# Gate-up groups of a feed-forward layer: the upper right product last, the next group's first split behind the result additions

## The chip, the cores and the metric

The kernel runs on one core of a Trainium2 chip. The metric is the device time of one execution in microseconds (us); lower is better. The core's engines work side by side, each through its own queue in order: TensorE (PE; its weight loads are shown as PEld), VectorE (DVE), ScalarE (ACT), GpSimd (POOL) and SyncE (SP). They wait for one another by semaphores. Matrix products are accumulated in PSUM, eight banks of 128 x 512 numbers; VectorE and ScalarE read and write these banks too. Operands lie in SBUF, and transfers from HBM are issued by SP and POOL.

## The reference

One layer of an encoder on x of 256 x 2048, all in float32:

```
x = x + 0.5 * post1(SwiGLU_1(pre1(x)))      # feed-forward, inner width 5632
h = pre_m(x);  p = h @ W_in                  # one projection
x = x + post_m(concat(HGRN2(p), attention(p)) @ W_out)
x = x + 0.5 * post2(SwiGLU_2(pre2(x)))      # feed-forward again

def swiglu(x, w_gate_up, w_down):
    gate, up = jnp.split(x @ w_gate_up, 2, axis=-1)
    return (jax.nn.silu(gate) * up) @ w_down
```

The change lies in `x @ w_gate_up`, a product of 256 x 2048 by 2048 x 11264, which is there twice, once for each feed-forward layer. With the gate and up halves read side by side, it is worked on in groups of columns.

## The kernel before, in words

**Numbers in two parts.** TensorE takes float32 operands in a rounded form. So each weight is split: ScalarE casts it to a rounded part h (L176), and VectorE subtracts this from the weight and leaves a rest l (L177). A product is then three matmuls, h by the large part of x, l by the large part, h by the small part (`three`, L441). A split of half a loaded weight tile is one cast and one subtraction of 128 x 1024. The h and l tiles come from pools of five buffers each, so a cast waits until TensorE is done with an older tile.

**Groups.** A group of `Gated` is 512 columns of gate and the same 512 of up, for all 256 rows and all 2048 inner places. There are NG = 11 groups to a layer, 0 to 10. Inside a group the inner places come in eight pairs u = 0 to 7 (two blocks of 128 each). A group has four results in four PSUM banks: c[m][n], where m is the upper or lower 128 rows and n is gate (left) or up (right).

**Plain pairs and seven-product pairs.** A plain pair needs eight block products, so 24 matmuls. Some pairs (`MIXED_IN`: u = 2, 4, 5, 6; in group 1 only 2 and 4) are worked on with seven block products instead of eight, by a scheme of sums and differences like Strassen's (`products`, L485). That is 21 matmuls, and they use sums of weight blocks (VectorE, L915 and L916, and an accumulating transfer that POOL issues in `prepare`, L901) and sums of x blocks (xs). Three of the seven products go straight into the result banks c[0][0], c[0][1] and c[1][0]; four go into four more banks: p1, p5 (tag pa), p6 and p7 (tag pb). All pairs of a group add into the same banks. The seven, in the order of the code, are: p1; c[0][0]; c[0][1], the upper right one; p5; p7; p6; c[1][0], the lower left one. The first needs its own split (prepared much earlier), the second and third need the split called `lower`, the fourth and fifth `upper`, the last two `last`.

**The boundary.** At the end of a group the four p banks have to be added into the four results. This is `boundary(g)` (L1101), for groups 1 to 9 of each layer, 18 times in the kernel. By then the last seven-product pair (u = 6) is queued on TensorE, and pair 7, a plain one, is still to do. Its products are queued bank by bank (`bank`, L1108): the six matmuls of a bank stand behind the addition into this bank. In order: ScalarE copies p1 (L1112); VectorE adds it to c[0][0] (L1113); L1116 and L1117 form sums with p6 and p7; L1118 adds to c[1][0]; L1121 and L1122 form a difference with p5 and add to c[0][1]; L1124 and L1125 do the same for c[1][1]. TensorE works the banks in the order c[0][0], c[1][0], c[0][1], c[1][1], and then begins pair 0 of the next group.

Between L1113 and L1116 the first half of the next group's pair 0 is split (`ahead = gated.splits(g + 1, 0)`, `next(ahead)`); the second half is split at the end, behind L1125.

**After it.** ScalarE computes silu of the gate results (L1039) and VectorE the product with the up results (L1044), spread over the next group's first pairs. In some groups (2 to 5 of each layer) finished tiles of this are stored to HBM (`put_away`), since they don't all fit; the stores stand in SP's queue among the loads.

**What sets the order.** All of this stands under a manual schedule: the order of the Python calls is the order of the queues. A weight tile's buffer is loaded again (`load_next`) when its last split is done; for pair 0 that is behind the second half.

In the text, the boundaries are numbered 0 to 17 in order of time: 0 to 8 in the first layer, 9 to 17 in the second.

Of the kernel before, what the change touches and what calls it, by code (L numbers as in the profile page):

```python
# [24 lines left out]
KT = D // P  # L25
# [12 lines left out]
def hymba_layer_kernel(  # L38
# [41 lines left out]
    def pa():  # L80
        return psum.tile([P, 512], F32, tag="pa", name=nm("pa"))

    def pb():
        return psum.tile([P, 512], F32, tag="pb", name=nm("pb"))
# [130 lines left out]
    last = {}  # L215
# [20 lines left out]
    def take(*a):  # L236
        take_hi(*a)
        take_lo(*a)
# [59 lines left out]
    def proj_T_pieces(w, c0, xt, slot, khs=(0, 1), parts=None):  # L298

        for i, kh in enumerate(khs):  # L300
# [26 lines left out]
            for n, (products, at) in enumerate(steps):  # L327
                products(*at)
                if n % 4 == 3:
                    yield  # L330
# [71 lines left out]
    class Blocks:  # L402
# [4 lines left out]
        ahead = None  # L407
# [74 lines left out]
            last = split_half(raw, 1)  # L482
            self.products(u, first, lower, upper, last)

        def products(self, u, first, lower, upper, last):  # L485

            if not self.p:
                self.p = [pa(), pa(), pb(), pb()]
            a, w = self.tiles[u], self.left_sums(u)

            def lhs(k, m):
                return [a[:, k, i, m * P : (m + 1) * P] for i in range(2)]

            def summed(j):
                return [w[:, j, i, :] for i in range(2)]

            def rhs(two, n):
                return [x[:, n * 512 : (n + 1) * 512] for x in two]

            for at, left, right in (  # L500
                (("p", 0), lhs(0, 0), first),
                (("c", 0, 0), lhs(1, 0), rhs(lower, 0)),
                (("c", 0, 1), summed(S4), rhs(lower, 1)),
                (("p", 1), summed(S1), rhs(upper, 0)),
                (("p", 3), summed(S3), rhs(upper, 1)),
                (("p", 2), summed(S2), rhs(last, 1)),
                (("c", 1, 0), lhs(1, 1), rhs(last, 0)),
            ):
                self.three(at, *left, *right)

        def fold(self):
# [78 lines left out]
    class Pairs(Blocks):  # L590
# [93 lines left out]
        def finish(self, mul, post, new_x=None, gain=None, lead=None):  # L684
# [45 lines left out]
            if gain is None:  # L730
# [8 lines left out]
                with tc.manual_schedule(engines=ordered):  # L739
                    products(0, 0, every)  # L740
                    squares(0, 0)
                    gains(0, 0)
                    products(0, 1, every)
                    squares(0, 1)
                    gains(0, 1)
                    products(1, 0, every)
                    squares(1, 0)
                    for q in range(4):
                        update(0, q)
                    in_place(0)  # L750
                    products(1, 1, every)
                    squares(1, 1)
                    in_place(1)
                    for q in range(4):
                        store(0, q)
                    update_aside(1, 0)
                    for q in (1, 2, 3):
                        update(1, q)
                        store(1, q)
                    store(1, 0)  # L760
# [82 lines left out]
    NG = DFF // 512  # L843
# [11 lines left out]
    class Gated(Blocks):  # L855
# [73 lines left out]
        def take(self, g, u):  # L929

            got = self.split_of.pop((g, u))
            del self.raws[g, u]
            first = self.firsts.pop((g, u), None)
            if first:
                self.products(u, first, *got)
                return ()
            hs, ls = zip(*got)
            return [
                (lambda k=k, m=m, n=n: self.plain(u, hs, ls, m, n, k))
                for k in range(2)  # L940
                for m in range(2)
                for n in range(2)
            ]
# [27 lines left out]
    def ffn(gated, w_dn, post_gain, again, gain=None, lead=None, aside=None):  # L971

        with ExitStack() as st:
# [9 lines left out]
            def room_for(tag):  # L983
                return work.tile([P, 512], F32, tag=tag, name=nm(tag))
# [97 lines left out]
            def some(steps, n):  # L1082
                for _ in range(n):
                    next(steps)

            pre_stats()
            last = KT // 2 - 1
# [13 lines left out]
            def boundary(g):  # L1101

                a, b = room_for("z"), room_for("s")
                c, (p1, p5, p6, p7) = gated.c, gated.p
                add = nc.vector.tensor_tensor
                rest_of = gated.take(g, last)

                def bank(m, n):  # L1108
                    for k in range(2):
                        rest_of[4 * k + 2 * m + n]()  # L1110

                nc.scalar.copy(a, p1)  # L1112
                add(c[0][0], c[0][0], a, ALU.add)  # L1113
                ahead = gated.splits(g + 1, 0)
                next(ahead)
                add(b, p6, a, ALU.add)  # L1116
                add(a, p7, b, ALU.add)  # L1117
                add(c[1][0], c[1][0], a, ALU.add)  # L1118
                bank(0, 0)
                bank(1, 0)  # L1120
                add(b, p5, b, ALU.subtract)  # L1121
                add(c[0][1], c[0][1], b, ALU.add)  # L1122
                bank(0, 1)
                add(b, p5, a, ALU.subtract)  # L1124
                add(c[1][1], c[1][1], b, ALU.add)  # L1125
                bank(1, 1)
                next(ahead)

            def first_pairs(g, waiting):

# [36 lines left out]
            with tc.manual_schedule():  # L1167
                gated.prepare(1, MIXED_IN[0])
                some(gated.splits(1, 0), 2)
                for g in range(1, NG):  # L1170
                    first_pairs(g, waiting)
                    for u in range(2, last - 1):
                        pair_ahead(g, u)
                    if g < NG - 1:
                        ahead = gated.splits(g, last)
                        some(ahead, 2)
                        gated.prepare(g + 1, MIXED_IN[0])
                        for one in gated.take(g, last - 1):
                            one()
                        boundary(g)  # L1180
                        waiting = units(gated.c, rest)
                        some(waiting, 2)
# [47 lines left out]
    def two_banks():  # L1230
        return [[pa(), pa()], [pb(), pb()]]

    gated = Gated(w_ffn1_gate_up[0], two_banks())
    xt = new_xt()
    gated.see(xt)
    with tc.manual_schedule():
# [5 lines left out]
        def taken(m, q, js=range(4)):  # L1242
            take(m, q, gain1, xt, banks[m, q], js)
# [3 lines left out]
        first = gated.source(0)  # L1247
# [120 lines left out]
    with ExitStack() as s2:  # L1368
# [227 lines left out]
        def gates(half):  # L1596

            sl = [pa(), pa()]
            for _ in proj_N_pieces(w_in, 4096 + half * 512, 512, xt, sl):
                side_step()  # L1600
            g = mid.tile([P, 2, 512], F32, tag="g", name=nm("g"))
            for m in range(2):
                by = rs2[:, m : m + 1]
                nc.scalar.activation(g[:, m, :], sl[m], AF.Sigmoid, scale=by)
                nc.vector.scalar_tensor_tensor(g[:, m, :], sl[m], by, g[:, m, :], ALU.mult, ALU.mult)
            return g
# [129 lines left out]
        for hp in range(4):  # L1736
            zf = headpair(2048 + hp * 256, "zf")
            if hp == 1:
                g = gates(0)
# [18 lines left out]
        g = gates(1)  # L1758
# [13 lines left out]
        gated = Gated(w_ffn2_gate_up[0], two_banks())  # L1772
# [80 lines left out]
```

## Time and profile before

| | |
|---|---|
| median of 3 runs | 1850.8 us (1848.57 to 1854.73) |
| the profiled execution | 1851.23 us; its span, first to last instruction, 1849.5 us |
| TensorE busy | 1816.7 us, 98% of the span |
| VectorE busy | 1628.2 us, 88% |
| ScalarE busy | 1127.2 us, 61% |
| moved by DMA | 422.42 MB, 228 GB/s on average |
| granted TensorE clock | 0.999 of full speed |

The gate-up groups with boundaries last from about 60 to 480 us in the first layer and from about 1185 to 1605 us in the second. How to read the rows: a group such as "DVE L177 TENSOR_TENSOR l<-raw,h" names the engine, the line, the operation, and what is written from what. In an answer in order of time, each row begins with its start and its length in us; xN means so many instructions like it, and square brackets give the idle time of this engine ahead of it and what ended it. In an answer on waits, the numbers are the sum, the count and the longest. A matmul's end is modelled, 0.39 us behind its start, while the next one starts 0.227 us behind it; so starts are compared here. The idle time that the profile gives for TensorE counts from such modelled ends, and is shorter than the delay of the start.

### The profile page before, as it was taken

The page shows a single profiled execution, that of the slowest core. Times are in us where ns is not written, and L with a number is a line of the kernel's source. Part 1 is how long each engine was busy: PE and PEld are TensorE (multiplying, and loading weights), DVE is VectorE, ACT ScalarE, POOL GpSimd, SP SyncE. Part 2 cuts the span into 40 slices and gives each one's busy share as a digit, 9 for nine tenths or more (in the row PEclk, how much of TensorE's full clock was granted, in tenths as well). Part 3 has the DMA queues.
Part 4 walks back from the last instruction along what each step waited for, and adds up shares of the span by engine and source line. Part 5 has one row for each costly group of instructions (what it writes and reads, how often), then busy time and mean ns, then how long its engine had stood idle before and what let it go on. Part 6 is the DMA issues. An engine that isn't in the chain of part 4 may idle for free.

```text
span 1849.5 us, 23264 instructions
## 1 busy us (share of the span) xinstructions
PE 1816.7 (98%) x8438; PEld 1504.2 (81%) x8438; DVE 1628.2 (88%) x2071; ACT 1127.2 (61%) x1492; POOL 114.3 (6%) x115
## 2 busy tenths in 40 slices
PE   9999999999999999999999999999999999999998
PEld 7877878888887888888888888878888778888886
DVE  7999999998999999477687788899999999999897
ACT  7565556655665557477587556555666556666563
POOL 1011111111000000000000000011111111000000
PEclk9999999999999999999999999999999999999999
DMA  8789999888756566656554456789999888865565
GB/s 298 228 219 275 274 268 256 247 244 251 272 186 226 196 248 211 208 175 181 166 171 148 169 212 245 220 237 262 272 272 254 255 246 237 262 236 206 183 237 183
DMA packets 200020, 422.42 MB, mean 228 GB/s; under 512 B 10984, under 2 KB 45888, under 8 KB 199136
## 3 DMA queue, kind: packets, MB, share of 16 engines
q1 hardware_dynamic: 178880, 380.95, 59.9%
q0 software_dynamic: 21024, 39.99, 12.9%
q8 instruction: 66, 1.08, 0.2%
q14 instruction: 50, 0.41, 0.1%
HBM read 408.29 MB, written 12.60 MB: 228 GB/s over the span
## 4 chain that ended last, share of the span: by engine, by line
PE 70%; DVE 14%; DMA 8%; ACT 4%; issue 3%; SPq 1%; POOL 0%; DVEq 0%; ACTq 0%; POOLq 0%
PE pa L441 28%; PE pb L441 25%; DVE l L177 8%; DMA raw<-in_w_ffn_gate_up_dram 6%; PE pa L309 5%; PE pa L314 3%; ACT h L176 3%; PE pa L364 2%; PE pa L363 2%; PE pa L362 2%; DMA raw<-in_w_ffn_down_dram 2%; DVE pb L1118 1%; DVE z L1117 1%; DVE pa L1113 1%; DVE s L1116 1%
## 5 line engine op out<-in xcount | busy, mean ns | idle before, releaser
L176 ACT CAST h<-raw 128x1024 fp32r<-128x1024 f32 (+1 forms) x861 | 846.7, 1013 | 454.2 <-PE pb L441 113.2
L177 DVE TENSOR_TENSOR l<-raw,h 128x1024 fp32r<-128x1024 f32 (+1 forms) x861 | 985.0, 1170 | 136.8 <-ACT h L176 105.5
L441 PE MATMUL pa<-h,xt 128*128 128x512 f32 x1104 | 387.5, 392 | 0.2
L441 PE MATMUL pb<-h,xt 128*128 128x512 f32 x952 | 341.1, 393 | 17.5 <-DVE pb L1118 17.5
L441 PEld LDWEIGHTS pa<-h,xt 128*128 128x128 f32 x1104 | 207.4, 188 | 44.3 <-DVE xt L232 0.6
L441 PEld LDWEIGHTS pb<-h,xt 128*128 128x128 f32 x952 | 178.6, 188 | 64.4 <-DVE pb L1118 25.1
L441 PE MATMUL pa<-l,xt 128*128 128x512 f32 x552 | 215.7, 391 | 0.0
L441 PE MATMUL pb<-l,xt 128*128 128x512 f32 x476 | 185.5, 390 | 0.0
L441 PE MATMUL pb<-h,ht 128*128 128x512 f32 x464 | 163.5, 390 | 0.0
L441 PE MATMUL pa<-h,ht 128*128 128x512 f32 x464 | 162.7, 389 | 0.0
L901 POOL DMA_DIRECT2D raw<-in_w_ffn_gate_up_dram x76 | 92.0, 1211 | 758.1 <-DVE l L177 709.1
L309 PE MATMUL pa<-xt,h 128*128 128x512 f32 x512 | 124.4, 392 | 0.2 <-ACT h L176 0.2
L441 PEld LDWEIGHTS pa<-l,xt 128*128 128x128 f32 x552 | 103.9, 188 | 20.6 <-DVE l L177 0.7
L309 PEld LDWEIGHTS pa<-xt,h 128*128 128x128 f32 x512 | 93.8, 188 | 18.6 <-ACT h L176 0.6
L441 PE MATMUL pa<-h,xs 128*128 128x512 f32 x304 | 105.9, 389 | 0.0
L441 PE MATMUL pb<-h,xs 128*128 128x512 f32 x304 | 105.9, 389 | 0.0
L441 PEld LDWEIGHTS pb<-l,xt 128*128 128x128 f32 x476 | 89.4, 188 | 17.1
L441 PEld LDWEIGHTS pa<-h,ht 128*128 128x128 f32 x464 | 87.1, 188 | 18.2
L441 PEld LDWEIGHTS pb<-h,ht 128*128 128x128 f32 x464 | 87.1, 188 | 18.1
L441 PE MATMUL pb<-l,ht 128*128 128x512 f32 x232 | 90.3, 389 | 0.0
L441 PE MATMUL pa<-l,ht 128*128 128x512 f32 x232 | 90.3, 389 | 0.0
L314 PE MATMUL pa<-xt,l 128*128 128x256 f32 x512 | 69.1, 285 | 0.0
(289 smaller groups left out, 2517.6 us busy)
## 6 DMA issues: line engine op xcount, KB each, us to landing
raw<-in_w_ffn_gate_up_dram SPq DMA_DIRECT2D x350, 512.0 KB, 5.3
raw<-in_w_ffn_down_dram SPq DMA_DIRECT2D x88, 1024.0 KB, 5.2
raw<-in_w_mix_in_dram SPq DMA_DIRECT2D x52, 1024.0 KB, 5.0
raw<-in_w_ffn_gate_up_dram POOLq DMA_DIRECT2D x76, 512.0 KB, 8.3
raw<-in_w_mix_out_dram SPq DMA_DIRECT2D x16, 1024.0 KB, 5.0
away<-ht SPq DMA_DIRECT2D x16, 512.0 KB, 6.6
ht<-away SPq DMA_DIRECT2D x16, 512.0 KB, 7.4
pg<-in_post_norm_ffn_dram SPq DMA_DIRECT2D x4, 512.0 KB, 6.8
```

The costliest lines, as they stand in the source:

```text
L176: nc.scalar.copy(hi, src)
L177: nc.vector.tensor_tensor(lo, src, hi.bitcast(F32), ALU.subtract)
L309: nc.tensor.matmul(slot[f], weights(hs, kk, f), xcol(xt, k), start=(k == 0), stop=(k == KT - 1))
L314: nc.tensor.matmul(slot[f][:, 0:T], weights(ls, kk, f), xcol(xt, kh * 8 + kk, 0), start=False, stop=False,)
L362: nc.tensor.matmul(dst, xh, h[:, o : o + n], start=(k == 0), stop=False)
L363: nc.tensor.matmul(dst, xh, l[:, o : o + n], start=False, stop=False)
L364: nc.tensor.matmul(dst, xl, h[:, o : o + n], start=False, stop=(k == KT - 1))
L441: nc.tensor.matmul(self.bank(at), lhs, rhs, start=(n == 1), stop=n in (ends, self.of[at]), skip_group_check=n > ends,)
L901: nc.gpsimd.dma_start(raw[:, 0:1024].rearrange("p (k c) -> p k c", k=2), self.source(u, g)[:, :, 1], accum_op=ALU.add,)
L1113: add(c[0][0], c[0][0], a, ALU.add)
L1116: add(b, p6, a, ALU.add)
L1117: add(a, p7, b, ALU.add)
```

## The change

Two things change places, and no instruction is added or removed.

- In the last seven-product pair of a group (u = 6, in groups 2 to 9), the upper right product, which was third of the seven, comes last. The others keep their order: p1, c[0][0], p5, p7, p6, c[1][0], c[0][1].
- In `boundary`, the split of the next group's first half, which stood between L1113 and L1116, comes behind the last of the additions, directly ahead of the split of the second half.

```diff
-        def products(self, u, first, lower, upper, last):
+        def products(self, u, first, lower, upper, last, order=range(7)):
...
-            for at, left, right in (
+            seven = (
                 (("p", 0), lhs(0, 0), first),
                 (("c", 0, 0), lhs(1, 0), rhs(lower, 0)),
                 (("c", 0, 1), summed(S4), rhs(lower, 1)),
...
                 (("c", 1, 0), lhs(1, 1), rhs(last, 0)),
-            ):
+            )
+            for i in order:
+                at, left, right = seven[i]
                 self.three(at, *left, *right)
...
             if first:
-                self.products(u, first, *got)
+                before_fold = g < NG - 1 and u == KT // 2 - 2
+                self.products(u, first, *got, (0, 1, 3, 4, 5, 6, 2) if before_fold else range(7))
                 return ()
...
                 nc.scalar.copy(a, p1)
                 add(c[0][0], c[0][0], a, ALU.add)
-                ahead = gated.splits(g + 1, 0)
-                next(ahead)
                 add(b, p6, a, ALU.add)
...
                 add(c[1][1], c[1][1], b, ALU.add)
                 bank(1, 1)
-                next(ahead)
+                some(gated.splits(g + 1, 0), 2)
```

In the changed file the lines of `boundary` lie lower: L1112 to L1113 become L1115 to L1116, and L1116 to L1125 become L1117 to L1126.

## The prediction

> **What bounds the kernel now.** I read the page first (busy time, slices, chain), then who waits for line L1118, then one group boundary in order of time, then stretches of groups.
>
> ```profile
> PE 1816.7 (98%) x8438; PEld 1504.2 (81%) x8438; DVE 1628.2 (88%) x2071; ACT 1127.2 (61%) x1492; POOL 114.3 (6%) x115
> ...
> PE   9999999999999999999999999999999999999998
> ...
> DVE  7999999998999999477687788899999999999897
> ...
> PE 70%; DVE 14%; DMA 8%; ACT 4%; issue 3%; SPq 1%; POOL 0%; DVEq 0%; ACTq 0%; POOLq 0%
> ```
>
> TensorE is the bound at 98%, and 70% of the chain that ended last is its work; VectorE has 14%. In the first and the last third, which hold the gate-up groups of the two feed-forward layers, VectorE is at 9 tenths as well. One of its lines there makes TensorE wait:
>
> ```profile
> L1118 DVE TENSOR_TENSOR pb<-pb,z x18: 700/700/700, 96.9 to 1565.7; 128x512 f32<-128x512 f32 x18
> ...
>   PE pb L441: 17.5, 18
> ```
>
> Each of the 18 boundaries stops TensorE once, until the lower left result has its addition (L1118). One boundary (number 5 of 0 to 17; 0 to 8 lie in the first layer) in order of time:
>
> ```profile
> 306.39 0.39 PE L441 MATMUL pa<-h,xt 128*128 128x512 f32 x1
> ...
> 308.67 1.05 ACT L176 CAST h<-raw 128x1024 fp32r<-128x1024 f32 x1
> ...
> 309.49 0.69 DVE L1113 TENSOR_TENSOR pa<-pa,z 128x512 f32<-128x512 f32 x1
> ...
> 309.99 1.05 ACT L176 CAST h<-raw 128x1024 fp32r<-128x1024 f32 x1 [0.26 <-PE pb L441]
> ...
> 310.09 1.22 DVE L177 TENSOR_TENSOR l<-raw,h 128x1024 fp32r<-128x1024 f32 x1
> ...
> 310.24 0.39 PE L441 MATMUL pb<-h,xs 128*128 128x512 f32 x1
> ...
> 310.92 0.39 PE L441 MATMUL pb<-h,xt 128*128 128x512 f32 x1
> ...
> 311.15 0.39 PE L441 MATMUL pa<-h,xt 128*128 128x512 f32 x1
> ...
> 311.22 0.68 DVE L1116 TENSOR_TENSOR s<-pb,z 128x512 f32<-128x512 f32 x1
> ...
> 312.74 0.70 DVE L1118 TENSOR_TENSOR pb<-pb,z 128x512 f32<-128x512 f32 x1
> ...
> 313.49 0.50 PE L441 MATMUL pb<-h,xt 128*128 128x512 f32 x1 [0.82 <-DVE pb L1118]
> ...
> 314.06 0.70 DVE L1122 TENSOR_TENSOR pa<-pa,s 128x512 f32<-128x512 f32 x1
> ...
> 315.00 0.39 PE L441 MATMUL pa<-h,xt 128*128 128x512 f32 x1
> ...
> 315.52 0.70 DVE L1125 TENSOR_TENSOR pb<-pb,s 128x512 f32<-128x512 f32 x1
> ...
> 315.58 0.69 ACT L1039 ACTIVATE z<-pa,scales 128x512 f32<-128x512 f32 x1 [4.54 <-DVE s L1124]
> ...
> 316.13 1.21 DVE L177 TENSOR_TENSOR l<-raw,h 128x1024 fp32r<-128x1024 f32 x1
> ...
> 316.37 0.40 PE L441 MATMUL pb<-h,xt 128*128 128x512 f32 x1
> ...
> 317.26 0.74 DVE L1044 SCALAR_TENSOR_TENSOR z<-pa,scales,z 128x512 f32<-128x512 f32 x1
> ...
> 317.77 0.39 PE L441 MATMUL pa<-h,xt 128*128 128x512 f32 x1
> ```
>
> The pair's 21 matmuls issue from 306.39 to 311.15: 0.227 us each. A result bank then takes six, 1.36 us. The upper left bank starts at 311.15, so the lower left one could start at 312.51; it starts at 313.49, 0.98 us late. VectorE runs without a break from L1113 on, and the next group's first split (310.09) stands in it ahead of L1116. That split isn't needed before 317.77.
>
> **The change, part by part.** Nothing is added or removed; seven products and eight VectorE operations change places.
>
> The split behind the additions: L1113 to the split is 0.60 us from start to start, the split to L1116 1.13. Taking it out brings L1116, L1117, L1118, L1121, L1122, L1124 and L1125 forward by 1.13, if their operands are there. L1118 then ends at 313.44 - 1.13 = 312.31, ahead of TensorE's 312.51, so this wait goes. The next banks start every 1.36: 313.87, where L1122 has ended at 314.76 - 1.13 = 313.63, and 315.23, where L1125 has ended at 316.22 - 1.13 = 315.09. The new group starts at 316.59 instead of 317.77. TensorE's ceiling is 1.18 and VectorE's 1.13; I take 1.13, since margins of 0.14 to 0.24 less semaphore time leave nothing over.
>
> The row and the Trainium skill differ slightly on this price. Its page "VectorE: DVE Perf Modes", section "The DRAIN you can't avoid", says that the next VectorE operation starts only when the one before has emptied the pipe. By that the removed split is worth its whole 1.22, capped by 1.18, and the sum below would be some 0.5 us larger; the trace does not quite agree: L1116 starts at 311.22, before 310.09 + 1.22.
>
> The product order: the sixth product's last matmul (310.24, ends 310.63) comes 0.68 earlier, to 309.95, before L1116's new start 309.49 + 0.60 = 310.09. The seventh (310.92, ends 311.31) ends at 310.63, before L1118's new 311.61. Without this half of the change L1116 would wait from 310.09 to 310.63, so 0.5 of the 1.13 hangs on it where VectorE is on time. The upper right product, now last, ends at 311.31 and is wanted at 314.06 - 1.13. TensorE's time is the same in any order. This half applies from the second boundary of each layer on (16 of 18); at the two others the pair is plain and its products lie far back.
>
> What is moved past what: the casts of the first two splits (308.67, 309.99) take the room of earlier operands, and in the new order wait for the fourth and the sixth product, ending near 310.4 and 311.8. ScalarE idles 4.54 before 315.58, and the split that reads the first now starts near 315.0: nothing. The split must end before the group's second matmul, at 316.59 + 0.23; it ends near 316.2. The second split stays at 316.13, so the load that reuses that buffer (SP) is issued as before, and POOL's accumulating loads and all VectorE work from 317.26 on keep their times. What is late next is therefore VectorE, against a TensorE that is 1.13 further.
>
> Does each group keep it? That depends on what lies between two boundaries. Stretches from L1113 to L1113, of one, four and three groups (columns: stretch, length, busy time and count of PE, PEld, DVE, ACT, POOL, then clock, DMA share, GB/s):
>
> ```profile
> 93.60:136.60 43.00, 41.66 (x188) 34.10 (x187) 40.00 (x49) 25.80 (x31) 4.81 (x4) 1.00 0.85 228
> 136.60:309.50 172.90, 168.43 (x753) 137.68 (x753) 159.41 (x190) 102.92 (x121) 19.35 (x16) 1.00 0.93 268
> 309.50:438.10 128.60, 126.13 (x565) 103.32 (x565) 118.78 (x139) 77.53 (x90) 14.52 (x12) 1.00 0.88 245
> ```
>
> ScalarE's waits for loads in the second of them, and then in the third (sum, times, longest):
>
> ```profile
> ACT h L176 <- DMA raw<-in_w_ffn_gate_up_dram: 24.0, 12, 3.9
> ...
> ACT h L176 <- DMA raw<-in_w_ffn_gate_up_dram: 2.6, 3, 1.0
> ```
>
> And a group of the third in order of time:
>
> ```profile
> 331.78 1.05 ACT L176 CAST h<-raw 128x1024 fp32r<-128x1024 f32 x1 [0.99 <-PE pa L441]
> ...
> 332.87 1.22 DVE L177 TENSOR_TENSOR l<-raw,h 128x1024 fp32r<-128x1024 f32 x1 [0.82 <-ACT h L176]
> ...
> 343.11 2.59 DVE L177 TENSOR_TENSOR l<-raw,h 128x1024 fp32r<-128x1024 f32 x2 [0.81 <-ACT h L176]
> ```
>
> In the third stretch a group takes 42.87 us and VectorE works 39.6 of it. Its idle (0.82, 0.81) is behind casts which wait for TensorE to free their buffers (331.78): it follows TensorE. With 41.7 us a group VectorE still has 2.1 to spare, so these groups pass the lead on. So does the first stretch (40.0 of 43.0), the group after boundary 0, and its like after boundary 9.
>
> In the second stretch, where results are stored to HBM beside the loads, casts wait 24.0 us for weights. The chain there is load, cast, VectorE without a break, boundary, next load, and TensorE's earlier start doesn't shorten it. Each boundary takes 1.13 out again, but such a group first takes back the lead that TensorE had from the boundary before. It leaves only VectorE's idle that follows TensorE after the last wait for a load:
>
> ```profile
> 148.80 1.22 DVE L177 TENSOR_TENSOR l<-raw,h 128x1024 fp32r<-128x1024 f32 x1 [2.45 <-ACT h L176]
> ...
> 214.20 2.59 DVE L177 TENSOR_TENSOR l<-raw,h 128x1024 fp32r<-128x1024 f32 x2 [0.40 <-ACT h L176]
> ...
> 300.24 2.59 DVE L177 TENSOR_TENSOR l<-raw,h 128x1024 fp32r<-128x1024 f32 x2 [0.24 <-ACT h L176]
> ...
> 1295.45 2.59 DVE L177 TENSOR_TENSOR l<-raw,h 128x1024 fp32r<-128x1024 f32 x2 [0.23 <-ACT h L176]
> ...
> 1338.30 2.59 DVE L177 TENSOR_TENSOR l<-raw,h 128x1024 fp32r<-128x1024 f32 x2 [0.63 <-ACT h L176]
> ...
> 1381.19 2.58 DVE L177 TENSOR_TENSOR l<-raw,h 128x1024 fp32r<-128x1024 f32 x2 [0.57 <-ACT h L176]
> ```
>
> Of the eight such groups (after boundaries 1 to 4 and 10 to 13), five have 0.40, 0.24, 0.23, 0.63 and 0.57; the other three have none (148.80 is a load's). Sum 2.07. Bounds for the eight: 0, if the store and load traffic grows denser with shorter groups, and 8 x 1.13 = 9.0, if loads move forward with the work.
>
> The sum: boundaries 0 and 9 give 1.13 each; each group after them adds what it passes on. Full: 2 boundaries + 8 groups (after 0, 5, 6, 7 and after 9, 14, 15, 16) = 10 x 1.13 = 11.3; load-paced: 2.1. Together 13.4 us. The profiled execution took 1851.23 (span 1849.5), so 1837.8; the runs' median, 1850.8, is 0.4 lower: 1837.4.
>
> **The rivals.**
> *All boundaries keep theirs.* 18 x 1.13 = 20.3, 1830.5. For it: many loads are issued when VectorE frees a buffer, so a part could come earlier. Against it: the 24.0 us of waits for loads.
> *VectorE and the loads take back more.* VectorE's share would rise from 92% to 95% (39.6 of 41.7), with accumulating loads between. If the eight load-paced groups give nothing and the eight others half, 2 x 1.13 + 4.5 = 6.8: 1844.0. Against it: the idle of 0.82 and 0.81 behind TensorE.
> *No change.* Every group needs room freed by TensorE (331.78). If the boundary's wait only mirrors scarce room, an earlier start would be waited off at the next buffer, and 1850.8 stays. Against it: a split stands in front of L1118, without idle between. The Trainium skill, "Perfetto Trace Analysis", section "Optimization Strategy", says that the same gap repeating on the engine that should be saturated can mean too little room for the next tile; by that reading this rival holds, and the trace does not bear it out here, since the wait ends with an addition.
> *Slower.* The first split is now behind L1125, and TensorE needs it two matmuls into the group. If it ended 0.62 late, TensorE would wait there instead; every us more is paid up to 18 times. It loses 0.3% when the split ends 0.62 + 1.13 + 0.31 late, by a late cast or addition: 18 x 0.31 = 5.6, 1856.4. Against it: the cast is done 3 us before, and L1125's operands lie ready.
>
> **How the numbers follow.** Forecast 0.58, all kept 0.12, taken back 0.18, no change 0.06, slower 0.06. What this kernel's runs can tell from no change is about 0.3%, 5.6 us. Faster by more than that: 0.58 + 0.12 and nearly all of "taken back", 0.85. Within: 0.09; slower: 0.06. The range goes from all kept (1830.5, rounded down) to taken back with a microsecond for the spread of the runs (1845); its ends hold the bounds of the load-paced groups (11.3 and 20.3 us).
>
> **What would show it.** Right: L1119 (once L1118) makes TensorE wait near zero at boundaries 5 to 8 and 14 to 17, whose groups take 41.7 us; the four groups after boundary 1 keep about 43; casts there still wait some 24 us for loads. Wrong: waits of TensorE behind L177 or the group's first split; groups of 42.9 after boundary 5; or those four groups shorter by 4 us or more in all (then all is kept).

## The result, and the profile after

The changed kernel took 1835.8 us (median of 4 runs, 1835.46 to 1840.23), and the kernel before, on the same chip, 1852.8 (4 runs, 1848.57 to 1855.65): a ratio of 0.9916, 95% interval 0.9889 to 0.9942. A second comparison, beside the last of the experiments, gave 1838.6 (6 runs, 1835.99 to 1844.24) against 1851.1, a ratio of 0.9936 (0.9922 to 0.995). The profiled execution took 1835.46, with a span of 1833.7 where before's was 1849.5: 15.8 us less. It is the fastest of its runs, as the profiled one of the second comparison was; the ten runs together have a median of 1837.7, where 1837.4 was forecast.

The page of the changed kernel: busy time, the chain that ended last, and two groups of instructions (busy and mean ns, then the idle time ahead of them).

```profile
PE 1815.3 (99%) x8438; PEld 1503.5 (82%) x8438; DVE 1626.8 (89%) x2071; ACT 1125.7 (61%) x1492; POOL 114.4 (6%) x115
...
PE 72%; DVE 15%; DMA 6%; ACT 3%; issue 3%; SPq 0%; POOL 0%; DVEq 0%; ACTq 0%; POOLq 0%
...
L176 ACT CAST h<-raw 128x1024 fp32r<-128x1024 f32 (+1 forms) x861 | 843.9, 1013 | 472.2 <-DMA raw<-in_w_ffn_gate_up_dram 92.4
...
L441 PE MATMUL pb<-h,xt 128*128 128x512 f32 x952 | 340.9, 393 | 2.6 <-DVE pb L1119 2.4
```

The busy times are those of before to within 1.5 us. What has gone is TensorE's idle time ahead of the lower left bank: 17.5 us before, 2.4 now. The addition into that bank, L1119 now, made TensorE wait at seven boundaries instead of 18:

```profile
L1119 DVE TENSOR_TENSOR pb<-pb,z x18: 699/700/700, 95.6 to 1550.0; 128x512 f32<-128x512 f32 x18
...
  PE pb L441: 2.4, 7
```

Boundary 6 of the changed kernel in order of time, VectorE first and then TensorE's first matmul of each bank and of the new group:

```profile
346.65 0.69 DVE L1116 TENSOR_TENSOR pa<-pa,z 128x512 f32<-128x512 f32 x1
347.25 0.68 DVE L1117 TENSOR_TENSOR s<-pb,z 128x512 f32<-128x512 f32 x1
...
348.76 0.70 DVE L1119 TENSOR_TENSOR pb<-pb,z 128x512 f32<-128x512 f32 x1
...
351.62 0.70 DVE L1126 TENSOR_TENSOR pb<-pb,s 128x512 f32<-128x512 f32 x1
352.22 2.35 DVE L177 TENSOR_TENSOR l<-raw,h 128x1024 fp32r<-128x1024 f32 x2
```

```profile
348.31 0.39 PE L441 MATMUL pa<-h,xt 128*128 128x512 f32 x1
...
349.67 0.39 PE L441 MATMUL pb<-h,xt 128*128 128x512 f32 x1
...
351.04 0.39 PE L441 MATMUL pa<-h,xt 128*128 128x512 f32 x1
...
352.43 0.43 PE L441 MATMUL pb<-h,xt 128*128 128x512 f32 x1
...
353.86 0.39 PE L441 MATMUL pa<-h,xt 128*128 128x512 f32 x1
```

L1117 follows L1116 after 0.60 us, where 1.73 lay between the same two before. The lower left bank starts 1.36 behind the upper left one, without a wait. The new group starts 7.21 us behind L1116 (346.65 to 353.86); at boundary 5 of the kernel before it was 8.28 behind L1113 (309.49 to 317.77). So a boundary gives 1.07 us.

Stretches from boundary to boundary (length, busy time of PE, PEld, DVE, ACT, POOL, then clock, DMA share, GB/s), and ScalarE's waits for loads in the second of them:

```profile
93.50:135.30 41.80, 41.60 (x187) 34.03 (x186) 39.84 (x48) 25.11 (x30) 4.81 (x4) 1.00 0.85 236
135.30:304.90 169.60, 168.71 (x756) 137.92 (x755) 158.94 (x190) 103.11 (x121) 19.34 (x16) 1.00 0.93 273
304.90:430.20 125.30, 125.21 (x564) 102.90 (x563) 118.69 (x139) 77.07 (x90) 14.53 (x12) 1.00 0.88 252
```

```profile
ACT h L176 <- DMA raw<-in_w_ffn_gate_up_dram: 28.8, 13, 3.9
```

The first and the third stretch take 41.8 us a group (before 43.0 and 42.87). The second, with the stores, takes 42.4 (before 43.2), and casts wait 28.8 us for weights in it instead of 24.0.

### The profile page after: what moved, and what is told of

Same layout as the page of the kernel before. It is cut to its first block, busy times and chain, and to the rows that moved or that the text cites. A ratio compares the mean times of both kernels' runs of the same rounds, so it can differ in the third digit from the quotient of the medians.

```text
span 1833.7 us, 23264 instructions
## 1 busy us (share of the span) xinstructions
PE 1815.3 (99%) x8438; PEld 1503.5 (82%) x8438; DVE 1626.8 (89%) x2071; ACT 1125.7 (61%) x1492; POOL 114.4 (6%) x115
## 3 DMA queue, kind: packets, MB, share of 16 engines
q8 instruction: 66, 1.08, 0.2%
## 4 chain that ended last, share of the span: by engine, by line
PE 72%; DVE 15%; DMA 6%; ACT 3%; issue 3%; SPq 0%; POOL 0%; DVEq 0%; ACTq 0%; POOLq 0%
PE pa L441 29%; PE pb L441 26%; DVE l L177 8%; PE pa L309 5%; DMA raw<-in_w_ffn_gate_up_dram 5%; PE pa L314 3%; PE pa L364 2%; PE pa L363 2%; PE pa L362 2%; ACT h L176 2%; DMA raw<-in_w_ffn_down_dram 1%; DVE raw L473 1%; DVE raw L917 1%; DVE xt L1012 0%; DVE la L177 0%
## 5 line engine op out<-in xcount | busy, mean ns | idle before, releaser
L441 PEld LDWEIGHTS pa<-h,ht 128*128 128x128 f32 x464 | 87.1, 188 | 18.2
```

The source lines that it names most:

```text
L441: nc.tensor.matmul(self.bank(at), lhs, rhs, start=(n == 1), stop=n in (ends, self.of[at]), skip_group_check=n > ends,)
```

## The experiments

Beside them the kernel before took 1851.6 us (15 runs) for the first four, 1851.1 (14 runs) for the next four and 1851.1 (11 runs) for the last three. A group's time is that from one addition into c[0][0] to the next.

**The split moved, the products in the old order.**

```diff
-                self.products(u, first, *got, (0, 1, 3, 4, 5, 6, 2) if before_fold else range(7))
+                self.products(u, first, *got, range(7) if before_fold else range(7))
```

> The split moved, the products in their old order. Theory (VectorE's queue position, and then the sixth product): L1116 may start 1.13 us earlier but must wait for the sixth product, which ends 0.54 later than that start where VectorE is on time. So boundaries 5 to 8 and 14 to 17 gain about 0.6 each instead of 1.13, VectorE shows idle of about 0.5 ahead of L1117 (once L1116), TensorE still waits about 0.4 there, and groups after boundary 5 take 42.3 instead of 41.8; boundaries 0 and 9, whose last pair is plain, gain in full. About 6 to 10 us faster than before, 1843 to 1847. Rival (the order of the products is idle decoration): as the whole change, about 1836, groups of 41.8.

1840.25 us (1838.63 to 1840.98), ratio 0.9937 (0.9925 to 0.995). It gained more than I expected, 11.3 us; in the profile, 2.9 of it came from the eight load-paced groups (344.9 to 342.0 us in all), of which the expectation said nothing. The mechanism was the expected one: at 11 of the 18 boundaries VectorE waited ahead of L1117 for the sixth product, 0.44 us on average. One of them in order of time:

```profile
1467.48 0.69 DVE L1116 TENSOR_TENSOR pa<-pa,z 128x512 f32<-128x512 f32 x1
1468.67 0.69 DVE L1117 TENSOR_TENSOR s<-pb,z 128x512 f32<-128x512 f32 x1 [0.50 <-PE pb L441]
```

**The products in the new order, the split left in front of the sums.** (The diff is against the changed kernel.)

```diff
                 add(c[0][0], c[0][0], a, ALU.add)
+                ahead = gated.splits(g + 1, 0)
+                next(ahead)
                 add(b, p6, a, ALU.add)
...
-                some(gated.splits(g + 1, 0), 2)
+                next(ahead)
```

> The products in their new order, the split left ahead of L1116. Theory: with the split in front, L1116 starts after the sixth product's end in either order, so TensorE waits as before, 0.8 by the profile at each boundary, and groups take 42.9: no change, within 0.2%, about 1851. Rival (the order carries the gain, since results are ready earlier): half or more of the gain, 1843 or less.

1855.55 us (11 runs, 1853.82 to 1858.06), ratio 1.0023 (1.0015 to 1.0032): a little slower, which neither theory had. The rows at boundary 6, ScalarE and then VectorE (in this file L1116 is the addition into c[0][0], and L1119 the first sum):

```profile
353.00 1.05 ACT L176 CAST h<-raw 128x1024 fp32r<-128x1024 f32 x1 [0.62 <-PE pb L441]
```

```profile
353.18 0.69 DVE L1116 TENSOR_TENSOR pa<-pa,z 128x512 f32<-128x512 f32 x1
354.09 1.23 DVE L177 TENSOR_TENSOR l<-raw,h 128x1024 fp32r<-128x1024 f32 x1 [0.21 <-ACT h L176]
355.23 0.68 DVE L1119 TENSOR_TENSOR s<-pb,z 128x512 f32<-128x512 f32 x1
```

The cast for the next group takes a buffer that TensorE frees, and in the new order TensorE frees it a product later. At boundary 5 of before this cast started 0.82 us ahead of the addition into c[0][0] (308.67 and 309.49), here 0.18. So the split behind it starts late, and from the addition to the first sum it is 2.05 us instead of 1.73. Groups take 43.25 us instead of 42.87. With the split at the end the same late cast costs nothing, since VectorE has eight additions to do first.

**Both halves split in front of the sums** (the kernel before, with one more split there).

```diff
-                ahead = gated.splits(g + 1, 0)
-                next(ahead)
+                some(gated.splits(g + 1, 0), 2)
...
-                next(ahead)
```

> The kernel before with both halves of the next group's pair 0 split ahead of L1116, so the suspected cost is doubled. Theory: each boundary's additions come another 1.13 us later and TensorE waits 1.13 more, 2.0 by the profile; groups after boundary 5 take 44.0; 18 x 1.13 = 20 less about 2 that load-paced groups hide: 16 to 20 us slower, 1867 to 1871. Rival (the wait mirrors scarce room, and where the split stands in the queue decides nothing): no change, 1851.

1877.26 us (1876.22 to 1880.67), ratio 1.0142 (1.0128 to 1.0155): 25.7 slower, more than expected. Of three groups in the third stretch:

```profile
315.23:447.23 132.00, 126.13 (x566) 103.41 (x565) 119.55 (x139) 77.42 (x90) 14.53 (x12) 1.00 0.85 239
```

44.00 us each, 1.13 above before: the price of a split from start to start, with nothing of it hidden. So the rival of scarce room fell. The load-paced groups pay the price too: six of the eight take 43.99 to 44.01, so there the late loads cost nothing more. Four groups (after boundaries 4, 9, 10 and 14) take 45.53 to 45.59 instead. The clock explains it: in the group after boundary 4 it is 0.96 on average (the third number from the end), in the next one 1.00, and in 3.5 us right behind TensorE's wait at boundary 4 it is 0.52:

```profile
269.67:315.23 45.56, 43.60 (x190) 35.67 (x189) 40.14 (x48) 26.16 (x31) 4.84 (x4) 0.96 0.88 255
315.23:359.23 44.00, 42.04 (x190) 34.47 (x189) 40.15 (x48) 26.02 (x31) 4.84 (x4) 1.00 0.85 239
274.80:278.30 3.50, 3.50 (x9) 2.74 (x10) 2.62 (x4) 1.34 (x3) 0.00 (x0) 0.52 1.08 294
```

TensorE's matmuls start some 0.43 us apart there instead of 0.227, and its busy time in the group is 1.56 us longer. The trace shows five such drops, the fifth behind boundary 8, and all four runs have a granted clock of 0.994, where every other run of this case has 0.997 or more. Five times 1.56 is 7.8 us. With 18 x 1.13 = 20.3, less the 2 that the load-paced groups no longer lose to loads, this makes some 26 (an estimate), near the 25.7 measured. TensorE's waits at the 18 boundaries are 1.95 to 2.48 us here; in the kernel before they are at most 1.6, and there the clock drops behind none. Why it dropped behind these five of the 18, no run shows. The Trainium skill, "VectorE: DVE Perf Modes", section "The DRAIN you can't avoid", would make a split cost its whole 1.22 where the next operation waits for an empty pipe; these groups don't agree, by 0.09. The same section says that a next operation which isn't held back starts earlier, and the prediction left this out.

**The changed kernel without the stores.** (One of eight a layer is kept.)

```diff
             def put_away(u):
+                if u:
+                    away[u] = away[0]
+                    return
```

> The changed kernel with one of the eight stores to HBM in each layer kept and the other seven left out (the fetches read the one stored tile instead, so the result is not the layer's). Theory (the eight slower groups are paced by loads behind these stores): waits of ScalarE for loads between boundaries 1 and 5 fall from over 20 us to a few, these groups take about 41.8, and some 4 to 5 us go: 1831. Rival (these groups are paced by VectorE, or the loads are slow for another reason, such as the accumulating loads): groups stay near 42.4, 1836.

1831.5 us (1830.91 to 1831.72), ratio 0.9891 (0.9875 to 0.9906). Four groups that were load-paced, and how long TensorE waited for L1122 (there the addition into the lower left bank):

```profile
135.90:303.08 167.18, 167.18 (x754) 137.93 (x753) 159.34 (x189) 104.20 (x121) 19.35 (x16) 1.00 0.91 255
```

```profile
  PE pb L441: 0.4, 2
```

41.8 us each, with TensorE busy all the time. So what the second stretch loses, it loses to the loads behind the stores.

**The kernel before without the stores.** The same edit in the kernel before.

> The kernel before with only one of the eight stores of each layer kept (the later fetches read that one tile, so the output isn't the layer's). Theory (the kernel before hides most of the stores' delay behind its own stall; its eight load-paced groups took 344.9 us in all, and 42.87 each would be 343.0): only 2 us faster than before, 1849 to 1850.5. With the changed kernel's 1831.5 without stores, the change is then worth about 18 us where no load is late. Rival (the stores cost the same in both): 4.3 us faster, 1847, and the change would be worth 16 there too.

1849.7 us (11 runs, 1848.33 to 1852.6), ratio 0.9992 (0.9983 to 1.0001), as expected: hardly faster, and not clear of the noise. The eight load-paced groups took 343.3 us in all instead of 344.9. So the kernel before hid all but some 1.4 us of the stores' delay behind its own stall. Without stores the change is worth 1849.7 - 1831.5 = 18.2 us.

**The stores behind pair 2, behind pair 3, and issued by POOL.** Nothing is left out. The three edits of the changed kernel:

```diff
-                if u == 5 and 1 < g <= AWAY // 2 + 1:
+                if u == 2 and 1 < g <= AWAY // 2 + 1:
```

> The changed kernel with the two stores of a group issued behind pair 2 instead of behind pair 5. Nothing is left out. With only one store to a layer the changed kernel took 1831.5 and its eight load-paced groups 41.8 us each, against 339.5 in all with the stores. Theory (a store issued behind pair 5 stands in SP's queue ahead of the loads that the next group's first pairs wait for): half or more of the 4.3 us comes back, 1831 to 1833.5, and the groups after boundaries 1 to 4 take 41.8 to 42.1. Rival (it is the traffic of 8 MB more, wherever it stands): 1835 to 1836, and the waits for loads move to other pairs.

```diff
-                if u == 5 and 1 < g <= AWAY // 2 + 1:
+                if u == 3 and 1 < g <= AWAY // 2 + 1:
```

> As the run before, with the stores behind pair 3. Theory of the queue's order: 1831 to 1833.5, as behind pair 2. Rival of the traffic: 1835 to 1836.

```diff
-                nc.sync.dma_start(away[u], hts[u].bitcast(F32).rearrange("p k i t -> p (k i t)"))
+                nc.gpsimd.dma_start(away[u], hts[u].bitcast(F32).rearrange("p k i t -> p (k i t)"))
```

> The changed kernel with the eight stores of each layer issued by POOL instead of SP, at the same places. Nothing is left out. Theory of the queue's order (SP's loads no longer stand behind a store): 1831 to 1833.5, groups after boundaries 1 to 4 of 41.8 to 42.1. Rival of the traffic: 1835 to 1836. A third way: POOL's accumulating loads come late behind the stores, VectorE's L177 of the seven-product pairs waits, 1838 or more.

Behind pair 2: 1835.71 us (1834.56 to 1836.82), ratio 0.9915 (0.9901 to 0.9929), no gain. Behind pair 3: 1830.18 (1828.46 to 1831.65), ratio 0.9885 (0.9871 to 0.9899). By POOL: 1830.19 (1828.29 to 1831.31), ratio 0.9884 (0.987 to 0.9898). In the last two all groups take 41.8 us. The loads of the next group's pair 1 at boundary 2 of the changed kernel and of that with the stores behind pair 3 (DMA issues: count, KB, median us to landing):

```profile
raw<-in_w_ffn_gate_up_dram SPq DMA_DIRECT2D x2, 512.0 KB, 9.6
```

```profile
raw<-in_w_ffn_gate_up_dram SPq DMA_DIRECT2D x2, 512.0 KB, 6.9
```

The traffic is the same, so its amount isn't the cause, but where the stores stand. Behind pair 2 it is another transfer that comes late, and VectorE waits for it directly (L917 adds weight blocks from a tile that POOL's accumulating transfer completes):

```profile
DVE raw L917 <- DMA raw<-in_w_ffn_gate_up_dram: 3.6, 4, 1.3
```

That row covers the first five groups; behind pair 3 no such wait is left. The transfer is the last accumulating one of a group, issued some 26 us into it: in the first four groups it lands after 9.5 to 10.3 us here, and after 5.9 to 6.2 with the stores behind pair 3. So the theory of the queue's order held for two of the edits and missed the third: moved to pair 2, the stores delay another transfer. This one stands in POOL's queue and not behind the stores in SP's; how they delay it, no run shows.

**The old order of the products, with the stores behind pair 3.**

```diff
-                self.products(u, first, *got, (0, 1, 3, 4, 5, 6, 2) if before_fold else range(7))
+                self.products(u, first, *got, range(7) if before_fold else range(7))
...
-                if u == 5 and 1 < g <= AWAY // 2 + 1:
+                if u == 3 and 1 < g <= AWAY // 2 + 1:
```

> The changed kernel with the seven products in the old order and the two stores of a group behind pair 3, where no load was late. Nothing is left out. The changed kernel with the stores there took 1830.2. Theory (the old order makes VectorE wait some 0.5 us ahead of L1117 at each boundary where it is on time, and with the loads in time that is all 16 with a seven-product pair): 16 x 0.53 = 8.5 more, 1838 to 1839.5, groups of 42.3. Rival (the order is worth what the run with late loads showed, 4.4): 1834 to 1835.

1837.8 us (6 runs, 1836.87 to 1841.99), ratio 0.9932 (0.992 to 0.9944). Who L1117 waits for:

```profile
L1117 DVE TENSOR_TENSOR s<-pb,z x18: 681/692/692, 94.3 to 1550.4; 128x512 f32<-128x512 f32 x18
...
  PE pb L441: 7.7, 16
```

VectorE waits 0.48 at each of the 16 boundaries that have a seven-product pair, and all groups between them take 42.3 us. The order is worth 7.5 to 8 us once no load is late (1837.8 against 1830.3). Where loads are late it is worth less, 1.7 to 4.4: 1840.25 against the changed kernel's two medians of 1838.6 and 1835.8, which other comparisons gave.

**The changed kernel and the stores behind pair 3, once more, on one chip.**

> The changed kernel once more, beside the run above: 1835 to 1836.5 by both. It is also the comparison for the runs with the stores behind pair 3 or issued by POOL.

> The changed kernel with the stores behind pair 3 once more, on the same chip as the changed kernel: 1830 to 1831, some 5.5 us below it.

The changed kernel 1838.56 (1835.99 to 1844.24), some 2 us above what was expected; the stores behind pair 3 1830.31 (1828.67 to 1830.57), ratio 0.9886 (0.9873 to 0.9898) to the kernel before. The slowest run of the second lies 5.4 us below the fastest of the first. So this kernel beats both. It has also lost much of the spread: its runs lie within 1.9 us here and 3.2 before, those of the changed kernel within 8.3 and 4.8. Late loads are a likely part of that: the changed kernel's eight paced groups took 339.5 us in one profile and 341.2 in the other; here they took 334.5 and 334.4.

Six instead of five buffers for h and l would test scarce room directly; that wasn't tried.

## Why the prediction was right, and where it was off

- **The split behind the additions.** Right. L1117 follows L1116 after 0.60, and the wait at the lower left bank goes. TensorE's ceiling of 1.18 was 0.1 too high: its banks and the new group started 1.36, 1.37, 1.39 and 1.43 apart (348.31 to 353.86), not 1.36 each. The rows of before show this too: 1.37 from 315.00 to 316.37 and 1.40 from there to 317.77. So a boundary gives 1.07 or 1.08 instead of 1.13, and the groups settle at 41.8, TensorE's own pace: without late loads nothing in the kernel goes below it.
- **The full terms, 11.3 us.** The profile's 15.8 less the 5.4 of the load-paced groups leaves 10.4 (11.5 in the second profile, 15.3 less 3.8).
- **The total, 13.4 us.** That the median of ten runs, 1837.7, lies so near the forecast is partly luck. Both profiles are of the fastest run and show more, 15.8 and 15.3, since the load-paced groups gave more than forecast. How much of it the slower runs kept, no trace shows.
- **The load-paced groups, 2.07 us: under-sized.** They took 344.9 us before and 339.5 after, 5.4 less (3.8 in the second profile). The mechanism was right. Boundary 2 shows it: from the addition into c[0][0] to the split that waits for the late load it is 12.45 us in the kernel before (180.58 to 193.03) and 12.44 in the changed one (177.74 to 190.18):

```profile
180.58 0.69 DVE L1113 TENSOR_TENSOR pa<-pa,z 128x512 f32<-128x512 f32 x1
...
193.03 1.23 DVE L177 TENSOR_TENSOR l<-raw,h 128x1024 fp32r<-128x1024 f32 x1 [1.41 <-ACT h L176]
```

```profile
177.74 0.69 DVE L1116 TENSOR_TENSOR pa<-pa,z 128x512 f32<-128x512 f32 x1
...
190.18 1.83 DVE L177 TENSOR_TENSOR l<-raw,h 128x1024 fp32r<-128x1024 f32 x2 [1.47 <-ACT h L176]
```

  Nothing is gained up to there, and all of it behind. Over the eight groups, VectorE's idle behind loads was 14.7 before and 15.1 after; its other idle went from 11.4 to 6.6, a gain of 4.8, and 1.1 came from instructions that follow one another more closely. The step that failed is the count of the idle that could be taken back: I took one row of each group and left out the shorter idles next to it. In the trace of before, VectorE's idles in these groups behind casts that wait for TensorE come to 4.4 us and not 2.07; in that of the changed kernel none is left. The groups after boundaries 11 and 12 were hardly load-paced: there two more waits followed TensorE, which the sum didn't have:

```profile
1317.03 2.96 DVE L177 TENSOR_TENSOR l<-raw,h 128x1024 fp32r<-128x1024 f32 x3 [0.96 <-ACT h L176]
...
1359.90 2.96 DVE L177 TENSOR_TENSOR l<-raw,h 128x1024 fp32r<-128x1024 f32 x3 [0.62 <-ACT h L176]
```

- **The product order.** Right in size: 0.5 of each boundary hangs on it where VectorE is on time, and 0.48 was measured, 16 times.
- **"Nothing" for the casts that wait longer.** Right, but only since the split moves as well. The order alone made the kernel 4 us slower through this wait. The two halves of the change aren't a sum: alone the order loses 4 us, and behind the other half it gains 1.7 to 8.
- **What would show it.** The wait at L1119 was to be near zero at boundaries 5 to 8 and 14 to 17. It was, but for 0.47 at boundary 14, where VectorE comes late out of a load-paced group. Groups were to take 41.7 (41.8); the four after boundary 1 to keep about 43 (42.4 on average, 3.3 shorter in all, under the 4 that would have meant that all is kept); casts there to wait some 24 us (28.8).
- **The rivals.** *All boundaries keep theirs* was the potential, not the result: 1830.5 forecast, and 1830.2 once the stores stood elsewhere. So near a match is partly luck, since 18 boundaries give 1.07 or 1.08 each, some 19.4, and the rest of the 20.9 is mostly what the stores had cost the kernel before. *The loads take back more* fell: of 8 x 1.08 = 8.6 in the load-paced groups they took back 3.2, and the other groups gave nothing back. *No change*, and the Trainium skill's "Perfetto Trace Analysis", section "Optimization Strategy", behind it: by too little room the wait would have come back, and it fell from 17.5 to 2.4 us instead. The gap was an order within VectorE's queue. Room did matter in another place: the 0.62 us that a cast waits for its buffer is what made the order alone a loss. *Slower*: the first split ended in time, and no row shows TensorE waiting for it.

## What to carry to other kernels

A split that is needed some us later shouldn't stand among the additions that the next bank waits for; its price is its start-to-start time, once for each boundary. When a stall is taken out, look at what it hid: here loads behind stores, which cost some 1.4 us before the change and 4 to 8 after it, and which another place for the stores gave back. And where two edits are made together, one can be a loss by itself and a gain behind the other, so neither is judged alone.

## What the runs showed of the hardware that I had not expected

The same stores cost some 5.5 us or nothing by their place alone: behind pair 5 the loads queued next landed after 9.6 us, with the stores elsewhere after 6.9. Issued by POOL, the stores cost nothing that shows, and POOL's accumulating transfers came in time as well (1830.19).

With both splits in front, TensorE waited some 2 us at each boundary, and behind five of the 18 waits the granted clock fell to about half for some 3.4 us. Each drop cost some 1.56 us more.
